# The second layer's projections as pairs of column blocks with seven half products each

## The chip, the cores and the metric

The kernel runs on one core of a Trainium2 chip. The metric is the device time of one execution in microseconds (us). The engines are named as in the profile: PE multiplies matrices (PEld loads its weights), DVE, ACT and POOL work on elements, SP issues the DMAs. TensorE's clock is given as granted, 1.00 being full speed.

## What is computed

One step of a trunk of two layers, on 512 prompt rows and 32 sample rows (T = 544 tokens), D = 1024. The first layer mixes tokens by an RWKV-7 recurrence, the second by differential attention; both add attention over 256 memory rows, gate all branches and project back. Cut to the second layer:

```
def diff_layer(x, mk, mv, k_past, v_past, layer_idx, norm_w, w_out, w_in, lq1, lk1, lq2, lk2, subln):
    h = rmsnorm(x, norm_w)
    q, k, v, qm, gate = jnp.split(h @ w_in, [MIX_W, 2 * MIX_W, 3 * MIX_W, 3 * MIX_W + MEM_W], axis=-1)
    ...
    attn = probs(q1, k1) - lam * probs(q2, k2)        # 12 heads of 128 columns
    o = rmsnorm(attn @ v_all, subln) * (1.0 - lam_init)
    y_mem = mem_attention(qm, mk, mv)                 # 4 heads
    out = jnp.concatenate([o, y_mem], axis=-1) * jax.nn.silu(gate)
    return x + out @ w_out, k, v
```

w_in (df_in) has 1024 x 7168 numbers: 56 blocks of 128 columns, 12 each for queries, keys and values, 4 for memory queries, 16 for gates. A last rmsnorm ends the trunk.

## The kernel before

All products are taken in three parts. A weight block W is split into whi (W rounded to the matmul's format, a cast on ACT) and wlo (W - whi, on DVE); the normed input into hh and hl in the same way. A product is then hh x whi + hl x whi + hh x wlo, summed in one bank of PSUM. hh and hl hold the input transposed: 8 chunks of 128 features, 544 tokens each.

`block` makes one column block: for each half of the tokens (TH = 272) it takes one of three banks (pool `psg`, tile ps_g) and issues 8 chunks x 3 parts = 24 matmuls of 128x272 by way of `steps`, then hands the bank to `evac`. Between the matmuls it issues `pieces`, generators that make the attention of a head in small steps (scores ps_s, transposes ps_aT, weighted sums ps_o). `weights`, `used` and `split` load (two DMAs of 256 KB into raw), cast and subtract a block ahead of its use; one whi and one wlo of 1024 rows have two buffers each.

`groups` walks through three groups of four heads: for each head a block of keys, of queries and of values, then the gates of the group, among them in two groups two blocks of memory queries and two of memory gates. Keys and values are copied from the bank to SBUF by ACT (tiles k, v); queries are split into qp by ACT and DVE straight from the bank; gates (tile sg) are made by ACT (tanh) and DVE (sg<-sg,ps_g) from the bank. kz is the keys' remainder. `diff_end` ends a group: it scales each head's result (ot<-ot,oss), transposes it and writes the gated result (og<-ps_oT,dv,sg).

Before the layer, `layer0` ends with the norm: hn = x1 times the scales (ps_r), hh by ACT, hl by POOL, while PE makes the second layer's memory keys and values (`mem_kv`, tiles memx, memz, memt). x1, the trunk's state, stays in SBUF.

After it, `w_out` makes the output projection from the 16 gated results o1[g]: hi by ACT, lo by DVE and POOL in turn. Six of them are split ahead of time (MADE = 6, by `aside`). Then come the residual and the last norm.

In this layer the order on an engine is that of the instructions as the building layer schedules them; the engines wait for each other by semaphores. Line 106 is a helper that issues every instruction of PE, DVE, ACT and SP, so the profile is read by tile names.

Of the kernel before, what the change touches and what calls it, by code (L numbers as in the profile page):

```python
# [17 lines left out]
P = 128  # L18
# [10 lines left out]
MH = 4  # L29
# [5 lines left out]
QB, KB = 2, 1  # L35
# [6 lines left out]
MADE = 6  # L42
# [55 lines left out]
class Queue:  # L98
# [5 lines left out]
    def __getattr__(self, name):  # L104
        issue = getattr(self.engine, name)
        return lambda *a, **k: self.trunk.tie(self, issue(*a, **k))  # L106


class Trunk:
# [183 lines left out]
    def split(self, raw):  # L293

        hi = self.wp.tile([P, KT, P], F32R, tag="whi", name="whi", bufs=2)
        lo = self.wp.tile([P, KT, P], F32R, tag="wlo", name="wlo", bufs=2)
        todo = []
        for q in range(2):
            k = slice(q * KT // 2, (q + 1) * KT // 2)
            todo.append((lambda k=k, q=q: self.ae.copy(hi[:, k], raw[q][:]), 0.0))  # L300
            todo.append((lambda k=k, q=q: self.ve.tensor_tensor(lo[:, k], raw[q][:], hi[:, k].bitcast(F32), ALU.subtract),
                         LATER))
        return (hi, lo), todo
# [752 lines left out]
    def gate_evac(self, n):  # L1056
        nc = self.nc
        sg = self.sg[n % SGB]
# [24 lines left out]
    def dest(self, g, sg):  # L1083

        return self.o1[g] if self.o1 else sg

    def put(self, g, t):
        self.out.add(g)
        if not self.o1:
            self.se.dma_start(self.oscr[g // 8][:, g % 8, :], t[:])  # L1090
# [146 lines left out]
    def mem_steps(self, st, i, h, p, two):  # L1237
# [78 lines left out]
        pool, tag = (self.psm, "m") if self.ordered else (self.psg, "g")  # L1316
        for c0, n, val in ((0, TP, mv), (TP, TS, cv)):
            po = pool.tile([P, 512], F32, tag=tag, name="ps_mo")
            for j in range(2):
                self.te.matmul(po[:, :n], val[:, j, :], pT[:, j, c0 : c0 + n], start=j == 0, stop=j == 1)  # L1320
            self.ve.scalar_tensor_tensor(g[:, c0 : c0 + n], sg[:, c0 : c0 + n], 0.5, po[:, :n], ALU.mult, ALU.mult)
# [3 lines left out]
    def fetch(self, p, g):  # L1325

        hi = p.tile([P, T], F32R, name=f"hi{g}")
        if self.o1:
            op, tag = self.lows.get(g, (p, f"lo{g}"))
            return hi, op.tile([P, T], F32R, tag=tag, name=f"lo{g}"), self.o1[g][:]  # L1330
# [5 lines left out]
    def gated(self, g, hi, lo, t):  # L1336

        self.ae.copy(hi[:], t)
        (self.nc.gpsimd if g % 2 and self.o1 else self.ve).tensor_tensor(lo[:], t, hi[:].bitcast(F32), ALU.subtract)  # L1339
# [14 lines left out]
    def w_out(self, i, p, order, consume, extra=None, o=None):  # L1354
# [5 lines left out]
        def fetch(n=1):  # L1360
            while left and len(came) < n and (self.o1 or left[0] in self.out):
# [11 lines left out]
        depth = 4 if self.o1 else NGATED  # L1373
# [66 lines left out]
    def layer0(self, mem):  # L1440
# [3 lines left out]
        self.o1 = None  # L1444
# [241 lines left out]
        with ExitStack() as ctx:  # L1686
            p = self.pool("wo0", 1, ctx=ctx)
            sums = p.tile([P, T], F32, name="sums")
# [32 lines left out]
            self.ahead = after[2:] + [(self.a[n][1], h * P) for n in ("w_mem_k", "w_mem_v") for h in range(MH)] + self.blocks1()  # L1721
# [27 lines left out]

            rs = self.token_rms((sums,), p)  # L1750
# [3 lines left out]
            for i in range(5):  # L1754
# [3 lines left out]
                c = i % 4 * P  # L1758
                self.te.matmul(pr[i // 4][:, c : c + n], self.ones[:], dg[:, P - n :], start=True, stop=True)
            for k in range(KT):  # L1760
                h = p.tile([P, T], F32, tag="hn", name="hn", bufs=HNB)
                for q, c, n in ((0, 0, TP), (1, TP, TS)):
                    self.ve.scalar_tensor_tensor(h[:, c : c + n], self.x1[:, k, c : c + n], self.nw[1][:, k : k + 1],
                                                   pr[q][:, :n], ALU.mult, ALU.mult)
                self.ae.copy(self.hh[:, k, :], h[:])
                nc.gpsimd.tensor_tensor(self.hl[:, k, :], h[:], self.hh[:, k, :].bitcast(F32), ALU.subtract)  # L1766
                next(kv, None)
            for _ in kv:
                pass
        mctx.close()  # L1770
        self.kctx.close()

    def blocks1(self):

        w = self.a["df_in"][0]
        cols = []
        for hg in range(3):
            for h in range(4 * hg, 4 * hg + 4):
                cols += [MIXW + h * P, h * P, 2 * MIXW + h * P]
            g = [3 * MIXW + 512 + h * P for h in range(4 * hg, 4 * hg + 4)]  # L1780
            if hg < 2:
                q, m = ([c + h * P for h in (2 * hg, 2 * hg + 1)] for c in (3 * MIXW, 3 * MIXW + 512 + MIXW))
                g = [g[0], q[0], g[1], g[2], q[1], g[3], m[0], m[1]]
            cols += g
        return [(w, c) for c in cols] + self.w_out_blocks(1)

    def layer1(self):
# [3 lines left out]
        op = self.pool("o1", 1)  # L1791
        self.o1 = [op.tile([P, T], F32, tag=f"og{g}", name=f"og{g}") for g in range(16)]
        order, made = list(range(8)) + [12, 13, 14, 15, 8, 9, 10, 11], {}
        self.lows = {g: (op, f"og{order[i - 2]}") for i, g in enumerate(order) if i > 1}
        with ExitStack() as ctx:
            with ExitStack() as c2:
# [15 lines left out]
                def aside():  # L1812
                    if pe:
                        made.update({g: self.gated(g, *self.fetch(pe[0], g)) for g in islice(early, 2)})
# [5 lines left out]
                self.groups(w, p, mp, nlam, aside, free)  # L1820
# [69 lines left out]
    def block(self, w, c0, evac, pieces=()):  # L1890

        pieces, steps = list(pieces), self.steps(self.weights(w, c0), evac)
        for i in range(6 * KT):
            while pieces and pieces[0][0] <= i:
                pieces.pop(0)[1]()
            next(steps)
        self.used()
        for _, fn in pieces:
            fn()

    def groups(self, w, p, mp, nlam, aside, free):

        late = []
        for hg in range(3):
            gr = self.diff_group(hg, p)
            heads = [self.diff_head(gr, j, p, nlam) for j in range(4)]
            sgs, fins, prev = [], [], None
            step = lambda it, *at: [(i, lambda: next(it, None)) for i in at]

            def gate(c0, pieces):  # L1910
                self.gates += 1
                sg, _, evac = self.gate_evac(self.gates)
                self.block(w, 3 * MIXW + 512 + c0, evac, pieces)
                return sg

            for j, (parts, it) in enumerate(heads):
                h = 4 * hg + j
                before = step(prev, 10, 20, 30, 40, 45) if j else late
                k, q, v = parts()
                self.block(w, MIXW + h * P, k, before)  # L1920
                if not j and hg == 2:
                    free()
                next(it)
                self.block(w, h * P, q, step(prev, 6, 18, 30, 42) if j else ())
                if j:
                    aside()
                if j == 3 and hg < 2:
                    mem = [self.mem_turn(1, 2 * hg + i, mp) for i in range(2)]
                    for _ in range(2):
                        next(mem[0][1])  # L1930
                self.block(w, 2 * MIXW + h * P, v, step(it, 6, 16, 28, 40))
                prev = it
            end = self.diff_end(gr, nlam)
            fin = lambda j, at: (at, lambda: end.send((j, sgs[j])))
            g0 = 4 * hg * P
            sgs.append(gate(g0, step(prev, 10, 20, 30, 40, 45)))
            if hg == 2:
                sgs.append(gate(g0 + P, step(prev, 6, 18, 30, 42)))
# [310 lines left out]
```

## Time and profile before

| | |
|---|---|
| time, median of 3 runs | 1372.9 us (1372.43 to 1373.5) |
| span of the profiled execution | 1371.9 us, 31923 instructions |
| PE busy | 1343.1 us (98%), 11893 matmuls |
| DVE busy | 932.7 us (68%) |
| ACT busy | 827.6 us (60%) |
| POOL busy | 379.0 us (28%), nearly all in the first layer |
| DMA | 139.45 MB, mean 102 GB/s |
| first layer's output projection begins, ends | about 668, 774 us |
| second layer's projections begin, end | about 800, 1259 us |

The profiled execution has a span of 1371.9 us from its first to its last instruction; its own time isn't listed apart, and the three runs lie 0.5 to 1.6 us above that span. Busy time on PE counts overlapped matmuls once; a mean in a group row is the duration of one instruction from start to end, which for matmuls is more than their distance in time. In a group's row, the number behind the second bar is the idle time of the engine ahead of these instructions, with what ended it.

### The profile page before, as it was taken

How to read it: one execution, taken by the hardware profiler on the slowest of the kernel's cores; microseconds unless marked ns; L12 is line 12 of the kernel's file. 1: busy time of each engine (PE TensorE's matmuls, PEld its weight loads, DVE VectorE, ACT ScalarE, POOL GpSimd, SP SyncE). 2: the span in 40 equal slices, each digit the busy share in tenths (PEclk: the TensorE clock that was granted, in tenths of full speed). 3: DMA queues.
4: the chain of work that ended last, by engine and by line, in shares of the span. 5: the costliest groups of instructions: out<-in, count | busy, mean ns of one | idle time of the engine just before them, and what ended most of it. 6: DMA issues, size and time to landing. Idle time of an engine off the chain costs nothing.

```text
span 1371.9 us, 31923 instructions
## 1 busy us (share of the span) xinstructions
PE 1343.1 (98%) x11893; PEld 1289.0 (94%) x11893; DVE 932.7 (68%) x2345; ACT 827.6 (60%) x2304; POOL 379.0 (28%) x841
## 2 busy tenths in 40 slices
PE   8999999999999999999999999999999999999997
PEld 6988899999999998988999999999999999999997
DVE  5776788888888888667734666775567747667443
ACT  5766777877778777656433466654566536665222
POOL 2128667766686666600000120000000001002000
PEclk9999999999999999999999999999999999999999
DMA  6452322333323332432644463333333323332321
GB/s 221 145 142 70 77 68 60 94 86 74 88 68 84 92 83 65 138 91 74 199 140 122 145 194 93 97 102 86 101 94 94 89 82 93 98 97 78 93 79 72
DMA packets 264036, 139.45 MB, mean 102 GB/s; under 512 B 57721, under 2 KB 252802, under 8 KB 263882
## 3 DMA queue, kind: packets, MB, share of 16 engines
q1 hardware_dynamic: 263818, 137.41, 35.7%
q8 instruction: 94, 1.54, 0.5%
q14 instruction: 60, 0.49, 0.1%
q10 hardware_dynamic: 64, 0.02, 0.0%
HBM read 111.12 MB, written 22.91 MB: 98 GB/s over the span
## 4 chain that ended last, share of the span: by engine, by line
PE 87%; DVE 5%; ACT 3%; POOL 2%; issue 1%; DMA 1%; SPq 1%; DVEq 0%; ACTq 0%; POOLq 0%
PE ps_g L106 60%; PE ps_c L106 5%; PE ps_s L106 2%; PE ps_o L106 2%; PE ps_at L106 2%; PE ps_v L106 2%; PE ps_mo L106 1%; PE ps_mm L106 1%; PE ps_w L106 1%; PE ps_aT L106 1%; POOL tm L868 1%; POOL u L870 1%; PE ps_yc L106 1%; PE ps_mt L106 1%; PE ps_wa L106 1%
## 5 line engine op out<-in xcount | busy, mean ns | idle before, releaser
L106 PE MATMUL ps_g<-hh,whi 128*128 128x272 f32 x1808 | 539.6, 299 | 1.0 <-DVE ats L106 0.7
L106 PE MATMUL ps_g<-hh,wlo 128*128 128x272 f32 x1808 | 534.7, 296 | 1.6 <-DVE wlo L106 1.5
L106 PE MATMUL ps_g<-hl,whi 128*128 128x272 f32 x1808 | 532.5, 295 | 0.6 <-DVE hl L106 0.3
L106 PEld LDWEIGHTS ps_g<-hh,whi 128*128 128x128 f32 x1808 | 341.1, 189 | 5.1 <-DVE ats L106 0.9
L106 PEld LDWEIGHTS ps_g<-hh,wlo 128*128 128x128 f32 x1808 | 340.6, 189 | 4.7 <-DVE wlo L106 2.5
L106 PEld LDWEIGHTS ps_g<-hl,whi 128*128 128x128 f32 x1808 | 341.1, 189 | 2.8 <-DVE hl L106 1.3
L106 DVE TENSOR_TENSOR wlo<-raw,whi 128x512 fp32r<-128x512 f32 x314 | 220.0, 711 | 122.3 <-ACT whi L106 118.9
L106 ACT CAST whi<-raw 128x512 fp32r<-128x512 f32 x314 | 188.9, 619 | 108.5 <-PE ps_g L106 61.4
L868 POOL TENSOR_TENSOR tm<-u,m 102x84 f32<-102x84 f32 (+23 forms) x341 | 145.6, 427 | 117.1 <-DMA m<-sc 67.1
L870 POOL TENSOR_TENSOR u<-u,tm 102x84 f32<-102x84 f32 (+23 forms) x341 | 150.4, 441 | 26.6
L106 PE MATMUL ps_g<-hi,whi 128*128 128x272 f32 x512 | 148.9, 291 | 0.0
L106 PE MATMUL ps_g<-hi,wlo 128*128 128x272 f32 x512 | 147.5, 288 | 0.5 <-DVE wlo L106 0.5
L106 PE MATMUL ps_g<-lo,whi 128*128 128x272 f32 x512 | 147.4, 288 | 0.0
L1339 POOL TENSOR_TENSOR lo<-og,hi 128x544 fp32r<-128x544 f32 x8 | 13.2, 1651 | 359.6 <-ACT hi L106 359.1
L106 PEld LDWEIGHTS ps_g<-hi,wlo 128*128 128x128 f32 x512 | 96.4, 188 | 0.8 <-DVE wlo L106 0.7
L106 PEld LDWEIGHTS ps_g<-hi,whi 128*128 128x128 f32 x512 | 96.4, 188 | 0.0
L106 PEld LDWEIGHTS ps_g<-lo,whi 128*128 128x128 f32 x512 | 96.4, 188 | 0.0
L106 ACT ACTIVATE pt<-ps_s,snm 128x128 f32<-128x128 f32 (+3 forms) x96 | 50.9, 531 | 41.8 <-DVE snm L106 41.6
L1766 POOL TENSOR_TENSOR hl<-hn,hh 128x544 fp32r<-128x544 f32 x8 | 12.5, 1566 | 211.2 <-ACT hh L106 211.2
L106 DVE SCALAR_TENSOR_TENSOR SB<-ps_c,dl,sd 64x64 f32<-64x64 f32 x168 | 47.4, 282 | 26.4 <-PE ps_c L106 21.1
L106 ACT COPY sv<-ps_c 64x64 f32<-64x64 f32 x192 | 39.5, 206 | 32.8 <-PE ps_c L106 30.9
L106 ACT ACTIVATE sg<-ps_g 128x272 f32<-128x272 f32 x64 | 25.2, 394 | 41.1 <-PE ps_g L106 38.3
(402 smaller groups left out, 2576.9 us busy)
## 6 DMA issues: line engine op xcount, KB each, us to landing
raw<-in_rw_in_dram SPq DMA_DIRECT2D x114, 256.0 KB
raw<-in_df_in_dram SPq DMA_DIRECT2D x112, 256.0 KB
raw<-in_w_out_dram SPq DMA_DIRECT2D x64, 256.0 KB
oscr<-sg SPq DMA_DIRECT2D x16, 272.0 KB
lo<-oscr SPq DMA_DIRECT2D x16, 272.0 KB
m<-sc SPq DMA_DIRECT2D x33, 128.0 KB
raw<-in_w_mem_v_dram SPq DMA_DIRECT2D x16, 256.0 KB
kh<-kh SPq DMA_DIRECT2D x24, 136.0 KB
```

The lines of the kernel that those rows point to most:

```text
L106: return lambda *a, **k: self.trunk.tie(self, issue(*a, **k))
L868: nc.gpsimd.tensor_tensor(tm[:, :n, :wd], u3[:, :n, kx : kx + 1].to_broadcast(sh), m3[:, kx : kx + 1, kx + 1 :].to_broadcast(sh), ALU.mult)
L870: nc.gpsimd.tensor_tensor(u3[:, :n, kx + 1 :], u3[:, :n, kx + 1 :], tm[:, :n, :wd], ALU.add)
L1339: (self.nc.gpsimd if g % 2 and self.o1 else self.ve).tensor_tensor(lo[:], t, hi[:].bitcast(F32), ALU.subtract)
L1766: nc.gpsimd.tensor_tensor(self.hl[:, k, :], h[:], self.hh[:, k, :].bitcast(F32), ALU.subtract)
```

## The change

The 56 column blocks become 28 pairs (`columns1`). A pair is one product of a weight of 2 x 2 quadrants (two column blocks A1., A2. by two halves of the features) with an input of 2 x 2 quadrants (two halves of the features by two halves of the tokens). It is made of seven products of quadrants in place of eight: 7 x 4 chunks x 3 parts = 84 matmuls of 128x272, where two blocks take 96. For this there are

- four sums of weight quadrants for each pair, on POOL (`pair_sum`, tile wsum, 128x512 each), before their split;
- seven splits for each pair (`pair_split`): seven casts on ACT, where there were four; four remainders wlo on DVE (as many as before), three on POOL;
- three sums of input quadrants for each chunk pair (tiles th, tl), made once in `norm1`;
- a combination of the seven banks (`after` in `pair`): one copy on ACT and seven additions of 128x272 on DVE for each pair, one operand in the bank, one in SBUF (tiles e, u, cx, k, v). What took a bank before (gates, queries) now takes the combined result in SBUF.

Room is made in SBUF: x1 is copied to DRAM (x1s) in `norm1` and read back before the output projection; its room holds ot, two more sg, e and u (in the rows below these all read x_10703). The gated results go to DRAM as in the first layer (`put`, oscr) and are read back by `fetch`; MADE becomes 3. whi and wlo are quads of 512 rows with four buffers each.

```
-MADE = 6
+MADE = 3
+PRODUCTS = (("A11", "B11"), ("A12", "B21"), ("S2", "T2"), ("S1", "T1"), ("S3", "T3"), ("S4", "B22"), ("A22", "T4"))
+WLOWS = (1, 3, 6)
...
+    def norm1(self, sums, mh, ml):
...
+            for k in range(half):
+                u = p.tile([P, 8, TH], F32, tag="hn", name="hn", bufs=2)
+                for t, j, q in ((1, k, 0), (0, k, 1), (3, k + half, 0), (4, k + half, 1)):
+                    self.ve.scalar_tensor_tensor(u[:, t], self.x1[:, j, q * TH : q * TH + TH], self.nw[1][:, j : j + 1],
+                                                 pr[q][:, :TH], ALU.mult, ALU.mult)
+                for j in (k, k + half):
+                    self.se.dma_start(self.x1s[:, j], self.x1[:, j])
+                for t, x, y in ((2, 0, 1), (5, 4, 2), (6, 4, 0), (7, 3, 5)):
+                    self.ve.tensor_tensor(u[:, t], u[:, x], u[:, y], ALU.subtract)
...
+    def pair_sum(self, n, s):
+        if n < len(self.cols1):
+            x, y, op = {"S1": ("A21", "A22", ALU.add), "S2": ("S1", "A11", ALU.subtract), "S3": ("A11", "A21", ALU.subtract),
+                        "S4": ("A12", "S2", ALU.subtract)}[s]
+            t = self.quads[n, s] = self.w1.tile([P, KT // 2, P], F32, tag="wsum", name="wsum", bufs=WSUMS)
+            self.nc.gpsimd.tensor_tensor(t[:], self.quads[n, x][:], self.quads[n, y][:], op)
+
+    def pair_split(self, n, i):
+        if n < len(self.cols1):
+            t, hi, lo = self.quads[n, PRODUCTS[i][0]], self.quad("whi"), self.quad("wlo")
+            self.ae.copy(hi[:], t[:])
+            (self.nc.gpsimd if i in WLOWS else self.ve).tensor_tensor(lo[:], t[:], hi[:].bitcast(F32), ALU.subtract)
+            self.quads[n, i] = hi, lo
...
+    def pair(self, e1, e2, pieces=()):
...
+        def give(to, v, x, bank, t=None):
+            if not to.dest and t is None:
+                t = self.dfp.tile([P, TH], F32, tag="cx", name="cx", bufs=2)[:]
+            d = to.dest(v) if to.dest else t
+            self.ve.tensor_tensor(d, x, bank, ALU.add)
+            if not to.dest:
+                to.emit(d, v)
+
+        def after(i, bank):
+            if i == 0:
+                self.ae.copy(e, bank)
+            elif i == 1:
+                give(e1, first, e, bank)
+            elif i == 2:
+                self.ve.tensor_tensor(e, e, bank, ALU.add)
+            elif i == 3:
+                self.ve.tensor_tensor(u, e, bank, ALU.add)
+            elif i == 4:
+                self.ve.tensor_tensor(e, e, bank, ALU.add)
+                give(e2, second, u, bank)
+            elif i == 5:
+                give(e1, second, u, bank, u)
+            else:
+                give(e2, first, e, bank, e)
+
+        for i, (_, xn) in enumerate(PRODUCTS):
+            self.pair_ahead(n, i)
+            hi, lo = self.quads.pop((n, i))
+            bank = self.psg.tile([P, 512], F32, tag="g", name="ps_g")[:, :TH]
+            for k in range(KT // 2):
+                xh, xl = self.side(xn, k)
+                for j, (wt, x) in enumerate(((hi, xh), (hi, xl), (lo, xh))):
...
+                    self.te.matmul(bank, wt[:, k, :], x, start=k == 0 and j == 0, stop=k == KT // 2 - 1 and j == 2)
+                    no += 1
+            after(i, bank)
...
+            for k in range(KT):
+                self.se.dma_start(self.x1[:, k], self.x1s[:, k])
             p = self.pool("wo1", 1, ctx=ctx)
```

`pair_ahead` splits the operand of the third product ahead before each product, and issues the sums of the next pair and the loads of the one after it at fixed places.

DVE's queue at the start of the second group of heads, before. The rows belong to one key block and one query block and the attention beside them:

```order
L106 TENSOR_TENSOR wlo<-raw,whi 128x512 x2
L106 TENSOR_TENSOR kz_12358<-k,kh 64x544 x2
L106 SCALAR_TENSOR_TENSOR qp<-ps_g,qp 64x272 x2
L106 TENSOR_TENSOR wlo<-raw,whi 128x512
L106 SCALAR_TENSOR_TENSOR qp<-ps_g,qp 64x272
L106 TENSOR_TENSOR wlo<-raw,whi 128x512
L106 SCALAR_TENSOR_TENSOR qp<-ps_g,qp 64x272
L106 MEMSET ps_s 64x64
```

The same place in the changed kernel, the first pair of the group (queries and keys of its first head):

```order
L110 TENSOR_TENSOR wlo<-rawx,whi 128x512
L110 TENSOR_TENSOR x_10703<-x_10703,ps_g 128x272
L110 TENSOR_TENSOR k<-x_10703,ps_g 128x272
L110 TENSOR_TENSOR x_10703<-x_10703,ps_g 128x272
L110 TENSOR_TENSOR wlo<-wsum,whi 128x512
L110 SCALAR_TENSOR_TENSOR qp<-x_10703,qp 64x272 x2
L110 SCALAR_TENSOR_TENSOR x_10703<-x_10703,ps_mo 128x512
L110 SCALAR_TENSOR_TENSOR x_10703<-x_10703,ps_mo 128x32
L110 TENSOR_TENSOR k<-x_10703,ps_g 128x272
L110 TENSOR_TENSOR kz_12558<-k,kh 64x544 x2
L110 TENSOR_TENSOR wlo<-wsum,whi 128x512
```

Between the remainders now stand the additions that empty the banks, and qp reads SBUF.

POOL's queue before, from the norm to the end of the layer's projections (lo are three of the results split ahead):

```order
L1766 TENSOR_TENSOR hl<-hn,hh 128x544 x8
L1804 MEMSET qs_12354 128x128
L1804 MEMSET qs_12355 128x128
L1809 MEMSET kz_12358 64x544 x2
L1809 MEMSET kz_12359 64x544 x2
L1339 TENSOR_TENSOR lo_17240<-og_12333,hi_17239 128x544
L1339 TENSOR_TENSOR lo_17602<-og_12335,hi_17601 128x544
L1339 TENSOR_TENSOR lo_17964<-og_12337,hi_17963 128x544
```

After, one pair out of 28 (the two remainders of raw are A12 and A22, that of wsum is S1):

```order
L1862 TENSOR_TENSOR wsum<-wsum,rawx 128x512
L1862 TENSOR_TENSOR wsum<-rawx 128x512
L1862 TENSOR_TENSOR wsum<-raw,wsum 128x512
L1869 TENSOR_TENSOR wlo<-raw,whi 128x512 x2
L1862 TENSOR_TENSOR wsum<-rawx,raw 128x512
L1869 TENSOR_TENSOR wlo<-wsum,whi 128x512
```

POOL, which had three operations in the whole stretch, has seven for each pair.

SP's queue at the turn to the output projection, before:

```order
L106 DMA out_dram<-vt 128x4x128
L106 DMA out_dram<-vs 32x512 x2
L106 DMA raw<-in_w_out_dram 128x4x128 x8
L106 DMA fw<-in_final_norm_w_dram 128x1024
L106 DMA raw<-in_w_out_dram 128x4x128 x23
```

and after:

```order
L110 DMA raw<-in_w_out_dram 128x4x128 x4
L110 DMA x_10703<-x1s 128x544 x2
L110 DMA oscr_12547<-sg_83 128x544
L110 DMA oscr_12547<-x_10703 128x544
L110 DMA x_10703<-x1s 128x544
L110 DMA oscr_12547<-x_10703 128x544
L110 DMA x_10703<-x1s 128x544 x2
L110 DMA oscr_12547<-sg_83 128x544
L110 DMA x_10703<-x1s 128x544 x3
L110 DMA fw<-in_final_norm_w_dram 128x1024
L110 DMA lo_19372<-oscr_12546 128x544
```

The last row is the first input of the output projection that isn't split ahead; it now stands behind the stores of the last gated results (oscr) and the reloads of x1.

309 lines of the change are left out of this document (190 added, 119 removed).

## Prediction

> **What bounds the kernel now.** I read the table of stages first: busy time of each engine in the norm between the layers, the second layer's projections with their attention, and the output projection with the tail.
>
> ```profile
> core 0: us, PE busy (x) PEld busy (x) DVE busy (x) ACT busy (x) POOL busy (x), PEclk, DMA share, GB/s
> 771.00:801.00 30.00, 28.69 (x232) 27.31 (x232) 26.69 (x53) 19.77 (x47) 13.87 (x13) 1.00 0.59 171
> 801.00:1259.00 458.00, 457.45 (x3613) 447.33 (x3613) 300.05 (x842) 267.34 (x798) 6.04 (x7) 1.00 0.35 97
> 1259.00:1372.00 113.00, 104.44 (x838) 103.65 (x836) 49.91 (x94) 32.44 (x64) 8.38 (x5) 0.97 0.27 83
> ```
>
> The change acts in the second row. There PE is busy for 457.5 of 458 us, DVE for 300, ACT for 267, POOL for 6. The list of PE's waits from 760 us to the end, and one piece of the chain that ended last, agree:
>
> ```profile
> PE ps_g L106 <- DVE wlo L106: 1.3, 3, 0.5
> 801.10 12.06 PE ps_g L106 x96
> ```
>
> PE waited 1.3 us in all, so matmuls taken away shorten this stage as long as PE stays the bound. One matmul costs not the 290 ns that the groups show as its duration (they overlap) but 12.06/96 = 0.1256 us.
>
> **The change part by part.** *Matmuls.* 56 column blocks with 48 matmuls each (2688) become 28 pairs with 84 (2352): 336 fewer, same shape, x 0.1256 = 42.2 us. If PE stayed the bound, the stage would take 415.8 us. That is 14.9 us for a pair; now two blocks take 458/28 = 16.4.
>
> *ACT.* 84 more casts of 128x512, and 28 copies of a bank in place of 48:
>
> ```profile
> L106 ACT CAST whi<-raw 128x512 fp32r<-128x512 f32 x111 | 67.3, 622 | 23.1 <-PE ps_g L106 20.6 <-ACT mp L106 1.6 <-ACT aT L106 0.5
> L106 ACT COPY k<-ps_g 128x272 f32<-128x272 f32 x24 | 9.3, 388 | 7.3 <-PE ps_g L106 7.3
> L106 ACT COPY v<-ps_g 128x272 f32<-128x272 f32 x24 | 9.1, 378 | 0.0
> ```
>
> 84 x 0.62 - 20 x 0.39 = 44 us: 267 becomes 311 of 416. It does not bind; cost zero, hidden by PE. If that cover were gone, ACT at 311 would still end ahead of both other engines.
>
> *DVE.* It keeps four of seven remainders wlo a pair (112, as before) and gains seven additions out of a bank for each pair, 196 in all, each 128x272 with one operand in SBUF and one in PSUM. The nearest rows are the same addition in the output projection, and two wlo back to back against one:
>
> ```profile
> L106 DVE TENSOR_TENSOR x<-ps_g,x 128x272 f32<-128x272 f32 x15 | 6.5, 442 | 28.8 <-PE ps_g L106 28.8
> 771.34 1.29 DVE L106 TENSOR_TENSOR wlo<-raw,whi 128x512 fp32r<-128x512 f32 x2 [2.05 <-ACT whi L106]
> 778.35 0.68 DVE L106 TENSOR_TENSOR wlo<-raw,whi 128x512 fp32r<-128x512 f32 x1
> ```
>
> Back to back an instruction costs 0.07 us less than it lasts, so 196 x 0.37 = 72.5 us: 300 becomes 372.6 of 416, before any wait.
>
> *POOL.* It is idle in this stage now and gets seven 128x512 operations a pair (four weight sums, three remainders), 196 in all. Its nearest rows:
>
> ```profile
> L792 POOL TENSOR_TENSOR rkk<-rkv 128x544 f32<-128x544 f32 x9 | 12.1, 1350 | 0.0
> L1766 POOL TENSOR_TENSOR hl<-hn,hh 128x544 fp32r<-128x544 f32 x8 | 12.5, 1566 | 211.2 <-ACT hh L106 211.2
> ```
>
> 1350 x 512/544 = 1.27 us each when undisturbed, 1.47 among DVE's work: 8.9 to 10.3 us of the 14.9 us of a pair. By itself that fits. But what it does to DVE does not come free. The timelines of the two stretches in which POOL runs such operations now:
>
> ```profile
> 781.80 5.17 POOL L1766 TENSOR_TENSOR hl<-hn,hh 128x544 fp32r<-128x544 f32 x3 [206.09 <-ACT hh L106]
> 782.77 1.20 DVE L106 TENSOR_TENSOR wlo<-raw,whi 128x512 fp32r<-128x512 f32 x1
> 784.07 1.68 DVE L106 TENSOR_TENSOR wlo<-raw,whi 128x512 fp32r<-128x512 f32 x1
> 785.67 0.73 DVE L106 SCALAR_TENSOR_TENSOR hn<-x,PB,ps_r 128x512 f32<-128x512 f32 x1
> ...
> 1132.98 0.72 DVE L106 TENSOR_TENSOR lo<-og,hi 128x544 fp32r<-128x544 f32 x1
> 1134.04 4.98 POOL L1339 TENSOR_TENSOR lo<-og,hi 128x544 fp32r<-128x544 f32 x3 [331.92 <-ACT hi L106]
> 1134.49 3.31 DVE L106 TENSOR_TENSOR lo<-og,hi 128x544 fp32r<-128x544 f32 x2 [0.79 <-ACT hi L106]
> 1137.72 1.84 DVE L106 TENSOR_TENSOR wlo<-raw,whi 128x512 fp32r<-128x512 f32 x1
> ...
> L106 DVE TENSOR_TENSOR wlo<-raw,whi 128x512 fp32r<-128x512 f32 x17 | 16.1, 972 | 3.3 <-ACT whi L106 3.3
> L106 DVE TENSOR_TENSOR memz<-memx,mo 128x256 f32<-128x256 f32 x4 | 2.2, 544 | 0.0
> 775.75 0.42 DVE L106 TENSOR_TENSOR memz<-memx,mo 128x256 f32<-128x256 f32 x1
> ```
>
> A wlo that starts under a POOL operation lasts 1.2 to 1.84 us in place of 0.68. An hn, which reads one operand from PSUM, keeps its 0.73. So a DVE instruction with both operands in SBUF stands still until the POOL operation is through. Price: from 771 to 801 us, 17 x (0.97 - 0.68) + 4 x (0.54 - 0.42) = 5.4 us for eight POOL operations, 0.68 each; at 1134 us (two lo of 0.72, one wlo) 5.1 - 2.1 = 3.0 us for three, 1.0 each.
>
> The Trainium skill ("SBUF — State Buffer", Who interferes with whom) says it as a rule: a DVE instruction with two SBUF inputs and a GpSimd instruction that reads SBUF exclude each other, and the one issued second fully blocks. This trace agrees (1.68 against 0.68 us), and by the rule alone, with perfect packing, the shared port would be taken for about 196 x 1.27 + 163 (next rows) = 412 us of the 416, an estimate: the 42 us would be kept only if no such instruction ever met another. I go by the measured price.
>
> How often DVE's queue offers such an instruction:
>
> ```profile
> L106 DVE TENSOR_TENSOR wlo<-raw,whi 128x512 fp32r<-128x512 f32 x112 | 78.1, 700 | 44.9 <-ACT whi L106 42.5
> L106 DVE SCALAR_TENSOR_TENSOR qp<-ps_g,qp 64x272 fp32r<-64x272 f32 x48 | 21.1, 439 | 7.2 <-ACT qp L106 6.0
> L106 DVE TENSOR_TENSOR kz<-k,kh 64x544 fp32r<-64x544 f32 x24 | 17.2, 717 | 0.4
> L106 DVE SCALAR_TENSOR_TENSOR sg<-sg,ps_g 128x272 f32<-128x272 f32 x31 | 13.5, 434 | 9.2 <-ACT sg L106 9.2
> L106 DVE SCALAR_TENSOR_TENSOR pt<-pt,srs 128x512 f32<-128x512 f32 x12 | 8.9, 745 | 0.0
> L106 DVE SCALAR_TENSOR_TENSOR pt<-pt,srs 128x384 f32<-128x384 f32 x12 | 7.4, 618 | 0.4
> L106 DVE SCALAR_TENSOR_TENSOR pt<-pt,srs 128x256 f32<-128x256 f32 x12 | 5.8, 484 | 0.4
> ```
>
> With the smaller forms of pt and mp these make 163 us, 44% of the 372.6 (qp and sg, which read a bank now, read the combined result in SBUF after the change, so they join). In the 30 us row the share was (17 x 0.68 + 4 x 0.42)/(26.7 - 5.4) = 62%. Scaled by the shares, 0.68 becomes 0.49. I take 0.6, between the two, because DVE will have hardly any idle time in which a POOL operation could run unmet. That is 196 x 0.6 = 118 us: DVE needs 372.6 + 118 = 491 us, and it sets the end of the stage in PE's place: +33 us against 458. Bounds: 0, when PE is the bound at 416 (-42), and 1.0, when DVE takes 569 (+111). The price turns into a loss above (458 - 372.6)/196 = 0.44. PE's first wait will be for a bank: a product fills one in 12 x 0.126 = 1.5 us (3.0 before), there are three as before, and its emptying stands in DVE's queue behind blocked remainders. ACT's exponentials, scores and transposes then come late behind PE.
>
> *Norm ahead of the layer.* DVE gets 16 subtractions of 128x272 (16 x 0.37 = 5.9 us) and four remainders of 128x816 (from 0.42 at 256 and 0.68 at 512 columns: about 1.0 each, 3.7), fewer small hn pieces and weight splits (-3), and about five more POOL operations at 0.68 (+3.4): +10 on 26.7 of 30 busy us. PE's own 28.7 us of memory keys and values runs alongside but waits for DVE's wlo. I take +8; ends 2 (PE's work covers the rest) and 12. The copies of x1 to DRAM (8 x 272 KB) go beside a DMA share of 0.59 and cost nothing unless the weights for the first pair come late behind them.
>
> *Turn to the output projection.* Before, six of the 16 inputs were split early and the others lay in SBUF. Now three are; the others come back from DRAM, and their loads stand on SP's queue behind the last gated head's store, the reloads of x1 and one load of 512 KB. Rows from the same pattern in the first layer (issue; cast that waited for its landing; rate around it):
>
> ```profile
> 681.13 0.35 SPq L106 DMA_DIRECT2D lo<-oscr  x1
> 685.98 0.65 ACT L106 CAST hi<-lo 128x544 fp32r<-128x544 f32 x1 [1.78 <-DMA lo<-oscr]
> 676.00:690.00 14.00, 14.00 (x114) 14.00 (x114) 8.06 (x14) 7.13 (x13) 0.00 (x0) 1.00 0.87 258
> ...
> L106 DVE TENSOR_SCALAR ot<-ot,oss 128x128 f32<-128x128 f32 x16 | 4.1, 279 | 0.0
> L106 DVE SCALAR_TENSOR_TENSOR og<-ps_oT,dv,sg 128x512 f32<-128x512 f32 x4 | 3.0, 743 | 0.0
> ```
>
> After the last product DVE still has the last sum, eight ot, three og, a wlo and small pieces of the last heads: about 5.5 us, with the overlaps taken off. Five issues on SP at about 0.5 make 2.5; landing 4.9; cast 0.65: 13.5 us. PE has 36 matmuls and some transposes meanwhile, 6 us. Three x1 reloads and the 512 KB ahead (1.3 MB at 258 GB/s, 5 us) can add to it. I take +9 of idle PE; ends 0 and 15. Behind it the inputs land every 1.1 us, faster than PE uses them (12 matmuls, 1.5 us).
>
> Sum: 1371.9 + 33 + 8 + 9 = 1422 of span. The median of the runs lies 1.0 us above the profiled span: 1423.
>
> **The rivals.** (a) PE stays the bound. POOL can be the one that waits; in the first layer it often is:
>
> ```profile
> 341.78 2.86 POOL L868 TENSOR_TENSOR tm<-u,m 102x84 f32<-102x84 f32 x1
> 341.97 0.67 DVE L106 TENSOR_TENSOR wlo<-raw,whi 128x512 fp32r<-128x512 f32 x1
> 342.57 0.71 DVE L106 SCALAR_TENSOR_TENSOR sg<-sg,bv 128x544 f32<-128x544 f32 x1
> ```
>
> There DVE ran at its usual speed and the short POOL operation took 2.86 us. POOL has 4 to 6 us to spare in each pair. This decides when a POOL operation costs DVE less than (415.8 - 372.6)/196 = 0.22 us. Then: 1372.9 - 42 + 17 = 1348, or up to 1356 with the port packed tightly but not perfectly. Against it: POOL's operations here hold on for 1.27 us, and the rows with such long ones (0.68, 1.0) show DVE as the loser.
>
> (b) A balance: 0.3 to 0.4 us each, DVE at 431 to 451, and the 17 us of norm and turn eat the rest: 1363 to 1383.
>
> (c) The dense price: 1.0 us each, as at 1134 us: 1372.9 + 111 + 17 = 1501. For it: DVE without idle time meets every operation. Against it: over half of DVE's work reads PSUM or one operand.
>
> (d) Norm and turn are hidden (2 + 0): the forecast falls to 1408.
>
> **How the numbers follow.** Forecast, with (d) and prices from 0.45 to 0.85: 0.63; (c) and beyond: 0.09; (a): 0.18; (b): 0.10, in equal parts below, within and above the resolution of about 0.2% (2.7 us), which is what runs of this kernel tell from no change. Faster 0.21, same 0.04, slower 0.75. The forecast's own range is 1380 (price 0.45, norm and turn mostly hidden) to 1475 (0.85). The 8-in-10 range leaves out about 0.1 at each end: 1350 (half of (a)) to 1478.
>
> **What would show each step.** Right: 28 x 84 matmuls at 0.126 us, but PE's share of the stage down to some 85 to 90%, its waits named "x" or "e" additions of DVE on ps_g; DVE above 90% busy; wlo with a mean near 1 us against 0.70; POOL operations of 1.3 to 1.6 us; a gap of PE of 5 to 12 us where hi<-lo waits for lo<-oscr. Wrong: wlo at 0.70 with POOL busy (no loss to the port), PE at 98% and a stage of about 416 us; or a long POOL row with short DVE rows beside it (rival a). A first wait elsewhere, on raw loads or on a whi of ACT, would make the mechanism wrong whatever the time.

## The result, and the profile after

The changed kernel takes 1466.1 us (median of 4 runs, 1464.3 to 1474.2), the kernel before 1373.2 us on the same chip (1372.4 to 1373.6): ratio 1.069, 95% interval 1.066 to 1.072, slower by 93 us. The profiled execution took 1464.3 us with a span of 1462.2. One execution in the experiments below, with the turn changed in the changed kernel, took 1820 us at a granted clock of 0.65 and is left out of that run's median.

The table of stages after the change (columns as in the prediction's first fence; norm, projections with attention, output projection and tail):

```profile
769.00:813.00 44.00, 33.80 (x248) 31.52 (x248) 41.29 (x72) 25.66 (x56) 24.80 (x14) 0.94 0.61 179
813.00:1334.00 521.00, 449.71 (x3251) 421.41 (x3251) 451.98 (x1016) 308.32 (x852) 261.96 (x200) 0.96 0.31 89
1334.00:1462.00 128.00, 108.94 (x849) 106.80 (x847) 58.09 (x119) 36.53 (x68) 10.56 (x7) 0.94 0.40 130
```

Against the rows of before: the projections 521 us in place of 458 (+63), their start at 813 in place of 801 (+12), the rest 128.2 in place of 112.9 (+15): together the 90 us between the two spans. The projections' matmuls do not begin all at once: 20 of them are done by 813, 7 by 801 before, so the start is later by some 10 us rather than 12. In the middle row no engine is full any more: PE 449.7 (86%), DVE 452.0 (87%), ACT 308, POOL 262. The number behind POOL's is the granted clock: 0.96, where it was 1.00.

What PE waited for in the projections (total, times, longest, in us):

```profile
PE ps_aT L110 <- DVE pt L110: 37.9, 27, 3.3
PE ps_s L110 <- ACT pt L110: 9.3, 12, 1.4
PE ps_oT L110 <- DVE x L110: 9.0, 8, 2.1
PE ps_saT L110 <- DVE ssb L110: 4.3, 2, 2.1
PE ps_kv L110 <- DVE k L110: 2.9, 1, 2.9
```

All of PE's waits in the stage add up to 72 us, and half of it is one wait: the transposes of the softmax (ps_aT) for pt, the last step of the softmax on DVE. The projections' own matmuls (ps_g) wait for under 1 us in all. One of the waits of 3.3 us, in the timelines of DVE, POOL and PE for the same stretch:

```profile
909.80 0.41 DVE L110 TENSOR_SCALAR pt<-pt,srs 128x384 f32<-128x384 f32 x1
910.24 1.38 DVE L110 SCALAR_TENSOR_TENSOR qp<-cx,qp 64x272 fp32r<-64x272 f32 x1
911.65 1.50 DVE L110 SCALAR_TENSOR_TENSOR pt<-pt,srs 128x384 f32<-128x384 f32 x1
```

```profile
910.01 1.32 POOL L1862 TENSOR_TENSOR wsum<-raw,wsum 128x512 f32<-128x512 f32 x1 [0.75 <-PE ps_g L110]
911.29 1.46 POOL L1869 TENSOR_TENSOR wlo<-raw,whi 128x512 fp32r<-128x512 f32 x1
```

```profile
909.73 0.29 PE L110 MATMUL ps_g<-hh,whi 128*128 128x272 f32 x1
913.31 0.88 PE L110 MATMUL ps_aT<-ident,pt 128*128 128x128 f32 x3 [3.29 <-DVE pt L110]
...
914.20 0.43 PE L110 MATMUL ps_g<-hh,wlo 128*128 128x272 f32 x1
914.43 0.43 PE L110 MATMUL ps_g<-hh,whi 128*128 128x272 f32 x1
914.66 0.43 PE L110 MATMUL ps_g<-hl,whi 128*128 128x272 f32 x1
```

A query remainder (qp, 0.44 us by the trace of before) stands under a POOL sum and ends just after it; the next instruction, the combination pt (0.62 us before), meets the next POOL operation, takes 1.50 us and ends 0.4 us after that one. PE, which has the transpose of this pt next in its order, stands for 3.29 us. And when it goes on, its matmuls start 0.23 us apart, not 0.127, until 916.8: the clock is at half. By the record of the granted clock it stood at half for 45.6 of the 521 us, and PE was busy in 43.9 of them: some 22 us lost. The Trainium skill ("TensorE: Matmul & The Clock Gate", What's actually happening) gives an idle window of about 3.4 us as what halves the clock; the half clock is as it says, but here gaps of 2.1 us were followed by it too (at 963 and 1149 us).

DVE's rows in the stage that are longer than before (mean in ns behind the comma):

```profile
L110 DVE TENSOR_TENSOR wlo<-wsum,whi 128x512 fp32r<-128x512 f32 x83 | 74.5, 898 | 12.7 <-ACT whi L110 12.0
L110 DVE TENSOR_TENSOR kz<-k,kh 64x544 fp32r<-64x544 f32 x24 | 22.8, 950 | 5.8 <-ACT kh L110 5.5
L110 DVE TENSOR_TENSOR srs<-srs,nlam 128x1 f32<-128x1 f32 x51 | 21.1, 413 | 0.4
L110 DVE TENSOR_SCALAR x<-x,oss 128x128 f32<-128x128 f32 x36 | 17.8, 530 | 0.0
L110 DVE SCALAR_TENSOR_TENSOR pt<-pt,srs 128x384 f32<-128x384 f32 x12 | 15.8, 1316 | 0.3
L110 DVE TENSOR_TENSOR cx<-x,ps_g 128x272 f32<-128x272 f32 x32 | 13.6, 426 | 4.5 <-PE ps_g L110 4.5
```

The additions out of a bank (last row) keep their price. All others work in SBUF alone: 0.90 for 0.70, 0.95 for 0.72, 1.32 for 0.62, and srs, a product one column wide, 0.41 for about 0.16. Also x<-x,oss, which has one tensor and a column of factors as inputs, takes 0.53 for 0.28.

### The profile page after: what moved, and what is told of

It reads as the page before. It is cut to its first block, busy times and chain, and to the rows that moved or that the text cites. A ratio compares the mean times of both kernels' runs of the same rounds, so it can differ in the third digit from the quotient of the medians.

```text
span 1462.2 us, 32137 instructions
## 1 busy us (share of the span) xinstructions
PE 1344.0 (92%) x11559; PEld 1269.9 (87%) x11559; DVE 1108.5 (76%) x2561; ACT 880.0 (60%) x2372; POOL 647.8 (44%) x1037
## 4 chain that ended last, share of the span: by engine, by line
PE 68%; DVE 19%; ACT 6%; issue 3%; DMA 3%; POOL 1%; SPq 0%; DVEq 0%; ACTq 0%; POOLq 0%
PE ps_g L110 45%; PE ps_c L110 5%; DVE pt L110 3%; DVE wlo L110 3%; DVE x L110 2%; PE ps_at L110 2%; PE ps_v L110 2%; DVE qp L110 1%; ACT whi L110 1%; DVE srs L110 1%; PE ps_s L110 1%; PE ps_o L110 1%; PE ps_aT L110 1%; PE ps_w L110 1%; ACT pt L110 1%
## 5 line engine op out<-in xcount | busy, mean ns | idle before, releaser
L110 PE MATMUL ps_g<-hh,wlo 128*128 128x272 f32 x1360 | 409.7, 302 | 3.5 <-DVE wlo L110 3.3
L110 PE MATMUL ps_g<-hl,whi 128*128 128x272 f32 x1360 | 409.8, 302 | 1.9 <-POOL hl L1813 1.4
L110 PE MATMUL ps_g<-hh,whi 128*128 128x272 f32 x1360 | 408.5, 301 | 0.9 <-DVE ats L110 0.7
L110 PEld LDWEIGHTS ps_g<-hh,wlo 128*128 128x128 f32 x1360 | 261.7, 193 | 5.1 <-DVE wlo L110 4.1
L110 PEld LDWEIGHTS ps_g<-hl,whi 128*128 128x128 f32 x1360 | 261.6, 193 | 3.9 <-POOL hl L1813 1.6
L110 PEld LDWEIGHTS ps_g<-hh,whi 128*128 128x128 f32 x1360 | 261.1, 192 | 4.2 <-DVE ats L110 0.9
L1869 POOL TENSOR_TENSOR wlo<-raw,whi 128x512 fp32r<-128x512 f32 x56 | 77.7, 1387 | 108.7 <-ACT whi L110 102.4
L110 PE MATMUL ps_g<-th,whi 128*128 128x272 f32 x336 | 102.2, 304 | 0.0
L110 PE MATMUL ps_g<-th,wlo 128*128 128x272 f32 x336 | 101.0, 301 | 0.5 <-POOL wlo L1869 0.5
L110 PE MATMUL ps_g<-tl,whi 128*128 128x272 f32 x336 | 100.0, 298 | 0.0
```

Of the source, the lines that this page charges most:

```text
L1869: (self.nc.gpsimd if i in WLOWS else self.ve).tensor_tensor(lo[:], t[:], hi[:].bitcast(F32), ALU.subtract)
```

## The experiments

The theory from these profiles: POOL's operations hold up DVE's SBUF instructions; the softmax's steps come late; PE, which meets them at fixed places in its order, stands, and then runs at half clock. The first rival: the seven additions and the longer way from a bank to queries, keys and gates do it, whatever POOL does. Times are medians, and each ratio stands against the kernel before on the same chip (1373.2 to 1373.8 us). "Stage" is the row of the projections, from 813 us on in the pair kernels and from about 800 in those built on the kernel before.

| run | us | ratio (95%) | stage, us | DVE busy in it |
|---|---|---|---|---|
| changed kernel | 1466.1 | 1.069 (1.066-1.072) | 521 | 452 |
| e1_no_pool | 1377.2 | 1.0035 (1.0021-1.0049) | 434 | 351 |
| e2_memset | 1393.5 | 1.0149 (1.0133-1.0165) | 447 | 369 |
| e3_all_dve | 1420.1 | 1.0349 (1.0328-1.0371) | 473 | 445 |
| e10_sums_pool | 1428.6 | 1.0396 (1.0379-1.0413) | 482 | 457 |
| e7_quarters | 1423.3 | 1.0361 (1.0345-1.0376) | 480 | 402 |
| e11_act | 1384.6 | 1.0079 (1.0064-1.0094) | 442 | 417 |
| e4_before_pool | 1446.4 | 1.0531 (1.0515-1.0547) | 533 | 402 |
| e9_pool_wlo | 1403.0 | 1.0213 (1.0198-1.0228) | 488 | 351 |
| e6_adds | 1382.8 | 1.0072 (1.0054-1.0090) | 466 | 355 |
| e12_no_pool_turn | 1371.7 | 0.9988 (0.9978-0.9997) | 434 | 351 |

**POOL's work left out.**

```
 def pair_sum(self, n, s):
+    if n:
+        self.quads[n, s] = self.quads[0, s]
+        return
 def pair_split(self, n, i):
+    if i in WLOWS: lo = self.still      # made once, of half the size
...
```

> The changed kernel with POOL's seven operations left out for every pair but the first: the weight sums and the three remainders of the first pair are used again by all later ones, so the products are of other numbers, and all else (28 x 84 matmuls, four remainders and seven additions on DVE, casts, loads, attention) stays. Theory (POOL's operations lock DVE's instructions that work in SBUF alone, DVE is late with the softmax, PE waits at the fixed places of the attention steps): DVE loses its 110 us of standing still, wlo<-rawx and wlo<-wsum go back to a mean of 0.69 us, PE's waits in the stage fall from 74 us to under 15, the stage takes 420 to 440 us and the whole 1360 to 1385 us. Rival (the seven additions and the longer way from a bank to queries, keys and gates make the chain late, whoever else works): wlo falls all the same, but the stage stays above 480 us and the whole above 1420 us.

1377.2 us, stage and remainder row:

```profile
813.00:1246.70 433.70, 426.51 (x3257) 405.29 (x3258) 351.04 (x1016) 307.58 (x854) 4.66 (x10) 1.00 0.37 105
```

```profile
L110 DVE TENSOR_TENSOR wlo<-wsumS,whi 128x512 fp32r<-128x512 f32 x84 | 57.9, 690 | 25.3 <-ACT whi L110 23.1
```

The theory holds, the rival falls: with the same matmuls, casts and additions, and DVE short of 189 POOL operations beside it, the stage is 87 us shorter. DVE is busy for 351 in place of 452 us: 0.53 us of standing still for each POOL operation. PE's waits fall from 72 to 9.5 us and the clock is back at 1.00. The 87 us are thus of two kinds: PE stands still for 7 in place of 71 us (stage less busy time), and its own busy time falls from 449.7 to 426.5, about what half clock had cost. The products are of other numbers here.

**POOL as busy, but writing only.**

```
-self.nc.gpsimd.tensor_tensor(t[:], self.quads[n, x][:], self.quads[n, y][:], op)
+for _ in range(3): self.nc.gpsimd.memset(t[:], 0.01)      # and so for its remainders
```

> The changed kernel with each of POOL's seven operations a pair (but for the first pair) replaced by three memsets of the same tile: POOL is busy about as long (near 1.5 us in place of 1.38), writes SBUF and sets and waits for the same semaphores, but reads nothing; the products are of other numbers. Theory (it is the reading of SBUF by POOL beside DVE's reading of two operands): as without POOL's work, wlo at 0.7 us, 1360 to 1395 us. Rival (any POOL work, its writes or its semaphores): DVE's rows stay long, 1440 us or more.

1393.5 us with POOL busy for 293 us of the stage, more than in the changed kernel. So it is POOL's reading that does most of it, not its semaphores. A memset is also shorter than the operation that it stands for (0.53 us), but the quarters below are as short and read, and they do lengthen wlo. What is left, 16 us, is in rows of one kind, the tensor_scalars. Two rows of this run, then the same two of the run without POOL's work:

```profile
L110 DVE TENSOR_SCALAR pt<-pt,srs 128x128 f32<-128x128 f32 x12 | 7.7, 643 | 0.0
L110 DVE SCALAR_TENSOR_TENSOR pt<-pt,srs 128x512 f32<-128x512 f32 x12 | 8.9, 741 | 0.1
```

```profile
L110 DVE TENSOR_SCALAR pt<-pt,srs 128x128 f32<-128x128 f32 x12 | 2.9, 241 | 0.0
L110 DVE SCALAR_TENSOR_TENSOR pt<-pt,srs 128x512 f32<-128x512 f32 x12 | 8.9, 744 | 0.1
```

Beside memsets the instruction with two tensors from SBUF loses nothing (0.74), and the one with a single tensor does (0.24 to 0.64). Both fit the Trainium skill ("SBUF — State Buffer", Who interferes with whom): two SBUF inputs collide only with a GpSimd instruction that reads SBUF, while a tensor_scalar in a two-port mode collides with any. That the tensor_scalars here ran in such a mode is not shown by a row.

**The same seven operations on DVE.**

```
-self.nc.gpsimd.tensor_tensor(t[:], ...)
+(self.ve if n else self.nc.gpsimd).tensor_tensor(t[:], ...)      # and WLOWS empty
```

> The changed kernel with the seven operations of each pair (but for the first pair's sums) moved from POOL to DVE: nothing else changes. Theory: a POOL operation costs DVE 0.58 us of standing still, and the same operation on DVE 0.61 us of work, so the two are worth the same: DVE 440 to 480 us busy, time within 20 us of 1466. Rival (it is the place and not the sum: a blocked instruction comes at the worst moment of the chain): 1430 us or less. Other rival (POOL took load off DVE after all): 1490 us or more.

```profile
813.00:1286.20 473.20, 439.15 (x3237) 408.13 (x3236) 445.07 (x1186) 310.24 (x850) 2.24 (x4) 0.99 0.34 98
```

The sum was right and the time was not: DVE is busy for 445 us, as much as when POOL took the work (452), but the stage is 48 us shorter. Here DVE is nearly full (94%). That it sets the end is borne out by the last experiment, in which 28 us less of DVE go with a stage 31 us shorter. In the changed kernel the same busy time stretches over 521 us. The first rival holds: an operation on POOL costs the whole (1466.1 - 1377.2)/189 = 0.47 us, the same one on DVE (1420.1 - 1377.2)/189 = 0.23. The way through the softmax shows the difference. From the reciprocal to the end of pt, a mean over the 48 softmaxes of the stage from their timelines, it takes 1.50 us in the kernel before, 2.90 in the changed one, 2.37 here, and 1.91 without POOL's work. It is a sign and not a price: in two runs further down it takes 2.34 us (quarters) and 2.30 us (DVE relieved) at stages of 480 and 442 us.

**Only the remainders moved to DVE** (WLOWS empty, the sums on POOL).

> The changed kernel with the three remainders of each pair moved from POOL to DVE, the four weight sums left on POOL. Theory (an operation on POOL costs the stage 0.46 us, by 1466 against 1377 us for 189 of them, and the same one on DVE 0.23 us, by 1420 against 1377): 1377 + 108 x 0.46 + 81 x 0.23 = 1445 us, between 1435 and 1455. Rival (the remainders, which come in the middle of the chain, do the harm, the sums not): 1425 us or less. Other rival (DVE is full and the locks now come on top): 1470 us or more.

```profile
813.00:1295.00 482.00, 436.26 (x3237) 410.62 (x3237) 457.38 (x1085) 310.60 (x850) 157.80 (x117) 0.98 0.34 97
```

```profile
PE ps_aT L110 <- DVE pt L110: 22.3, 19, 2.6
```

1428.6 us, below the 1445 of the linear sum and near its first rival (1425 or less). Taking 81 remainders off POOL gives back 37.5 us, 108 sums only 8.5 more. On DVE's busy time a POOL operation costs about as much as ever: (457.4 - 351.0 - 81 x 0.61)/108 = 0.53 us, or 0.61 us if a remainder on DVE is taken at the 0.50 that the run before gives, (445.1 - 351.0)/189. What differs is whom it hits. Taking for each DVE instruction its excess over the median of its form in the run without POOL's work, pt loses 23.7 us in 26 instructions in the changed kernel and 5.8 us in 6 here. That PE still waits 22.3 us for pt has another reason, which was not tested by itself: DVE is busy for 95% of this stage, as in the run with all seven on DVE, and pt stands in its queue. Why the remainders meet pt more often was not separated. In the changed kernel's stage POOL's idle time ahead of them ends mostly with a cast of ACT (113.5 us), that ahead of the sums with a remainder of DVE (83.4 us).

**POOL's operations cut into quarters** (four of 128x128 in place of one of 128x512).

```
+for c in range(4):
+    self.nc.gpsimd.tensor_tensor(t[:, c : c + 1], ..., op)
```

> The changed kernel with each POOL operation of 128x512 of the pairs cut into four of 128x128, the same numbers. Theory (a DVE instruction waits for the POOL operation that it meets, so a short one holds it for a short time): POOL's operations take 0.4 to 0.5 us, wlo<-wsum falls from 0.90 to 0.75 us or less, time 1390 to 1435 us. Rival (POOL goes on from one piece to the next without letting DVE in, or each piece locks anew): wlo stays at 0.90 or rises, 1455 us or more.

```profile
L1872 POOL TENSOR_TENSOR wlo<-raw,whi 128x128 fp32r<-128x128 f32 x222 | 112.6, 538 | 31.4 <-ACT whi L110 31.4
```

1423.3 us, 43 less for the same work, though POOL is busy for 398 us in place of 262: a quarter takes 0.54 us, more than a quarter of 1.38, and wlo<-wsum still has a mean of 0.76 us (0.69 without POOL's work). DVE's standing still goes to (401.7 - 351.0)/189 = 0.27 us per original operation. The instruction that is met waits for one POOL instruction, not for the whole row of them.

**POOL's operations added to the kernel before.** Twice 182 of 128x512, first raw - whi, then a finished wlo with itself:

```
+for q in range(3 + self.extra[0] % 2):      # in split, for 52 blocks
+    self.nc.gpsimd.tensor_tensor(self.spare, raw[q % 2][:], hi[:, k], ALU.subtract)
```

> The kernel before, with 3.5 POOL subtractions of 128x512 added for each of the first 52 column blocks (182 in all), raw minus whi into a spare tile that nobody reads; each holds raw and whi a little longer. Theory: the lock alone costs DVE 0.4 to 0.6 us for each, 70 to 110 us, so that DVE's 300 us become 370 to 410 of 458; PE stays the bound with a few waits for the softmax: 1373 to 1395 us. Rival (the lock as such, through the chain of the attention, is enough): 1420 us or more. Rival (POOL yields, DVE loses nothing): wlo at 0.70 us and 1373 us.

> The kernel before, with the 182 POOL operations of 128x512 for the first 52 column blocks once more, now sums of a finished wlo half with itself into a spare tile: they wait for DVE's remainder, hold no raw buffer, and no other engine waits for them. Theory (the lock on DVE alone makes the chain late): DVE stands still for 0.4 to 0.6 us for each operation and the time is 1425 to 1460 us, as when raw and whi were read. Rival (in that run it was raw buffers given back late): 1395 us or less.

```profile
800.00:1333.00 533.00, 485.49 (x3618) 464.02 (x3617) 402.35 (x843) 268.16 (x800) 288.10 (x192) 0.97 0.29 84
```

```profile
800.00:1288.00 488.00, 470.24 (x3620) 452.26 (x3619) 351.34 (x842) 268.11 (x799) 218.66 (x191) 0.99 0.32 91
```

+73 us in the first, against an expectation of 0 to 22 and as its first rival says (1420 us or more); +29 in the second, between theory and rival. DVE loses 102 us in the one (0.56 each) and 51 in the other (0.28 each); in the second a POOL operation starts just when DVE is through with a remainder, and meets fewer. In both DVE is far from full (75 and 72%) and PE has its matmuls of before, and still the stage grows. So a sum of DVE's time cannot give the cost. The first also gave raw buffers back later (the loads on SP's queue waited 166 us for POOL). Its trace shows no cost of that: ACT's casts of raw waited for no load, and had less idle time ahead of them than before (17.9 against 23.1 us).

```profile
L106 ACT CAST whi<-raw 128x512 fp32r<-128x512 f32 x112 | 68.1, 624 | 17.9 <-PE ps_g L106 15.1 <-issue 2.6
PE ps_o L106 <- DVE ot L106: 23.6, 9, 3.2
```

PE waited 0.5 us for a weight in all, and most for ot, the copy of a head's result out of its bank. That copy reads PSUM and is not held up itself; it stands in DVE's queue behind others that are.

A third form, with POOL reading the layer's input and a one-column copy on ACT to keep step, came to 1517.5 us (1425 to 1450 were expected) and tells nothing of how POOL holds up DVE:

> The kernel before, with the same 182 POOL operations of 128x512, now on two parts of the layer's input (hh and hl, which stay where they are) into two spare tiles in turn, so that no weight buffer is held by them; a copy of one column on ACT for each column block keeps them in step. Theory (DVE's instructions that stand behind a POOL operation delay the chain DVE - PE - ACT, and no sum is full): the locks cost DVE 90 to 110 us as in the run that held the weights, and the time is 1425 to 1450 us again. Rival (that run lost its 73 us because POOL held whi and raw, so that casts came late): 1395 us or less.

```profile
L106 ACT COPY tick<-og 128x1 f32<-128x1 f32 x52 | 9.9, 191 | 153.2 <-POOL og L308 152.5
```

The copies were issued ahead of ACT's other work, and ACT stood 152.5 us for POOL.

**DVE's additions alone, in the kernel before.**

```
+for _ in range(1 if self.extra[1] % 4 == 0 else 2):      # behind each bank's evac
+    self.ve.tensor_tensor(self.more, self.more, ps[:, :TH], ALU.add)
```

> The kernel before, with 182 additions of 128x272 added on DVE, one operand in the bank and one in SBUF, two for a bank (one for every fourth): what the pairs add on DVE, without POOL's work. Theory (work of DVE that nothing holds up fits in its idle time): DVE's 300 us in the stage become 365 to 375 of 458, PE's waits stay under 10 us, 1373 to 1385 us. Rival (DVE's added work is late for the softmax as POOL's locks are): 1405 us or more.

```profile
801.00:1267.00 466.00, 460.92 (x3608) 447.71 (x3608) 354.52 (x1022) 265.56 (x796) 5.90 (x7) 1.00 0.34 95
```

DVE +54 us for 182 additions (0.30 each), time +9.5: most of it hidden. Plain work on DVE fits in its gaps. POOL's locks of nearly the same total, the 51 us of the run on a finished wlo, cost 29 us.

**The turn to the output projection.** Reads of the results ahead of most reloads of x1, first in the changed kernel, then in the one without POOL's work:

```
-for k in range(KT): self.se.dma_start(self.x1[:, k], self.x1s[:, k])
...
 products = self.w_out(1, p, order, consume, o=made)[0]
+for k in range(KT): self.se.dma_start(self.x1[:, k], self.x1s[:, k])
```

> The changed kernel with the first four reads of the gated results issued ahead of most reloads of x1 and of the load of the last norm's weights, at the turn to the output projection. If the 9.3 us that PE waits there for hi is the landing behind those loads: the wait falls to 2 to 5 us and the time by 4 to 8 us, to 1458 to 1462 us. Rival (the wait is set by the stores of the last gated results or by the reading itself): 1466 us as before.

> The changed kernel without POOL's work, as in the first experiment (the first pair's sums and remainders are used again), and with the reads of the gated results ahead of most reloads of x1 at the turn. If PE's wait at the turn is the landing behind those loads: 1377 less 4 to 7 us, 1370 to 1373 us, and a wait for hi under 4 us. Rival (the time is only moved to a later wait for reloads or results): 1377 us.

In the changed kernel PE's wait for hi fell from 9.3 to 2.7 us, but the time did not follow: 1468.6 us, the median of three runs, ratio 1.0683 (1.0650 to 1.0717). In the profiled execution the stretch from the projections to the end is 4 us shorter (124 for 128), but the stage ahead is 11 us longer. PE's waits in it are the 72 us of before; the granted clock is 0.93 in place of 0.96. Without POOL's work, where the stage is steady, the time follows:

```profile
1247.50:1372.00 124.50, 109.36 (x848) 106.40 (x846) 57.76 (x117) 36.75 (x68) 11.07 (x7) 0.97 0.41 134
```

```profile
PE ps_g L110 <- ACT hi L110: 2.9, 1, 2.9
```

1371.7 against 1377.2 us; in the profiled executions the stretch from here to the end is 4.3 us shorter (128.8 to 124.5).

**DVE relieved by ACT.** All seven operations on DVE, the scaling and the copy of the heads' results and the scaling of the second softmax on ACT, the turn as above:

```
-self.ve.tensor_scalar(on[:, t, :], on[:, t, :], ss[...], None, ALU.mult)
+self.ae.activation(on[:, t, :], on[:, t, :], AF.Copy, scale=ss[...])
-self.ve.tensor_copy(ot[:, t, :], po[:, :P])
+self.ae.copy(ot[:, t, :], po[:, :P])
```

> The changed kernel with all seven operations of a pair on DVE, and three of DVE's own moved to ACT, which has 160 us to spare in the stage: the scaling of each head's result (48 of 128x128), its copy out of the bank (48 of 128x128) and the scaling of the second softmax (48 of 128 to 512 columns); and with the reads of the gated results ahead of the reloads at the turn. Theory (with POOL out of the way DVE is the bound of the stage at 94%): DVE loses 47 us there, the stage falls from 473 to 435 to 450 us, the whole from 1420 to 1380 to 1395 us. Rival (the chain DVE - ACT - DVE, now with more changes of engine, sets the stage): 1405 us or more. To beat the kernel before it would have to come under 1370 us.

```profile
813.00:1255.00 442.00, 428.47 (x3231) 404.16 (x3230) 416.75 (x1052) 348.27 (x980) 1.51 (x3) 1.00 0.37 105
```

1384.6 us: the time is as the theory says, though DVE lost only 28 of the 47 us expected (445 to 417). It is the best full version of the pairs, yet 0.8% slower than the kernel before. No version found beats that kernel. The run without POOL's work and with the better turn, which leaves out work that a full version must do somewhere, reaches 1371.7 us, 0.1% faster. So there is hardly anything to win this way here.

## Why the prediction was right, and where it was not

Forecast 1423 us, measured 1466. The direction and the place were right; the size was 50 us for 93. That 1466 lies within the range is in part luck: the upper part of the range was there for a higher price of POOL's operations, which did not come, and the time came from waits that the sum does not have. With DVE's measured 452 us in place of 491 the same working gives 1373 - 6 + 17 = 1384 us.

- *Matmuls.* 336 fewer at 0.1256 us: right; the two traces have 2688 and 2352 of them, at the usual distance wherever nothing holds them. But the bound of 415.8 us was too good: even without POOL's work the stage took 433.7, with 9.5 us of waits. Rival (a), 1348 to 1356, was thus out of reach: without any lock the whole is 1377.
- *ACT, zero.* Right: 308 of 521 us (forecast 311).
- *DVE's additions.* 0.43 us from start to end. Back to back priced at 0.37, which made 372.6 us for DVE without locks; the run without POOL's work shows 351.
- *POOL's lock.* 0.6 us for each operation, 118 us: measured 0.53, 101 us for 189 (without the first pair's). POOL's rows are 1.30 to 1.45 us (forecast 1.27 to 1.47). The share of instructions that can be hit was taken too small (the scaling of pt and of the heads' results is missing in it), but the value taken was nearly right. wlo's mean is 0.80 to 0.90, not "near 1 us".
- *"DVE 491 us sets the end": the step that failed.* DVE needed less, 452 us, and the stage took 521. The sum of an engine's time is the stage's time only if that engine is never idle, and DVE idled for 69 us. An instruction of 0.6 us that ends 0.9 us late holds the softmax; PE stands in its order ahead of the transposes, ACT behind PE, DVE behind ACT. With the same work on DVE alone, the step would have been nearly right: 445 of 473 us. The chance given to a higher price (rival c) named the wrong lever: not 1.0 us for each lock, but 0.53 us at places where others wait.
- *PE's first wait on a bank.* Wrong: the wait for pt makes 37.9 us, banks under 1 us. That the softmax comes late was said, as a consequence only; it is the mechanism.
- *The clock.* Not in the prediction: 45.6 us at half clock in the stage, some 22 us.
- *Norm +8 (2 to 12):* measured +12 at the stage's edge, some 10 by the matmuls done. Its rows show what was named, dearer than priced: DVE's 16 subtractions of 128x272 (hn) take 0.73 us each (forecast 0.37), its remainders of 128x816 (tl) 1.53 (forecast 1.0), beside POOL's weight sums and hl.
- *Turn +9 (0 to 15):* measured +15, with the wait for hi as forecast at 9.3 us. The reloads ahead of the reads were part of it, about 4 us; the rest, half clock behind the wait among it, was not separated.

Of the 43 us missing, 30 are in the projections (63 for 33), 6 in the turn and 4 in the norm; the other 3 are the median's distance from the profiled span (3.9 us for 1.0).

## What to carry to other kernels

Work handed to POOL cost DVE here about half a microsecond for each 128x512 operation that reads SBUF (0.28 to 0.61 by arrangement), and what that cost the kernel depended on which DVE instruction was met. In the changed kernel, where some of these are steps that PE waits for, it was twice the price of doing the work on DVE. Where engines trade work in fixed orders, look at which instructions others wait for, not only at each engine's sum. Cutting POOL's operations into quarters (1423.3 us) brought nearly as much as moving them to DVE (1420.1).

## What was not expected of the hardware

- A multiplication of one column (srs, 0.15 us) takes up to 1.24 us beside POOL's operations: the size of an instruction does not protect it.
- POOL's memsets hold up DVE's tensor_scalar from SBUF (0.24 to 0.64 us at 128x128) but not its instructions with two tensors (0.74 us both times).
- Four POOL operations of 128x128 cost DVE half as much standing still as one of 128x512 (0.27 against 0.53 us), though POOL is busy with them 1.5 times as long (398 against 262 us).
- In the changed kernel's stage, 9 of the 11 gaps of PE of 2.1 to 3.3 us were followed by 3 to 7 us at half clock (0.23 us from matmul to matmul), and 2 of the 18 gaps of 0.9 to 2.0 us.
